# Dealing the next quarter's modulation out among the column groups of the first projection's tiles

## The chip, the cores and the metric

The kernel runs on one core of a Trainium2 chip. The metric is the device time of one execution in microseconds (us); lower is better. The engines named below are TensorE (PE), its weight loads (PEld), VectorE (DVE), ScalarE (ACT), GpSimd (POOL) and SyncE (SP), whose queue issues nearly all loads.

## The reference, cut to what matters

One block of a streaming encoder over 256 positions of 2048 channels. What the change touches is its beginning: the modulation vectors and the first projection.

```python
c_act = jax.nn.silu(c)
mod = c_act @ w_ada[l] + b_ada[l]                        # (2048) @ (2048, 6*2048)
sh_m, sc_m, gt_m, sh_f, sc_f, gt_f = split(mod, 6)
h = rms_norm(x, g_norm_mix[l]) * (1 + sc_m) + sh_m
proj = h @ w_in[l]                                       # conv B | conv C | conv h | q lat | kv lat | key
...                                                      # short convolution, latent attention, w_out
x = x + gt_m * (merged @ w_out[l])
h2 = rms_norm(x, g_norm_ffn[l]) * (1 + sc_f) + sh_f
x = x + gt_f * peer_ffn(h2, ...)                         # retrieval over 16384 experts
return rms_norm(x, g_final)
```

All of it is float32. The kernel numbers the modulation vectors 0 to 5 in the order of the split: 0 is the mixer's shift, 1 its scale.

## The kernel before

Positions lie along the free axis (256 columns), channels along the partitions, in 16 tiles of 128. A weight tile is 128 x 2048 float32 (1 MiB). Its product is exact to float32 by three matmuls: ACT writes a rounded copy `hwin` (L198), DVE the remainder `lwin` (L199), and PE multiplies hi by hi, hi by lo and lo by hi. `rwin`, `hwin` and `lwin` are the raw, high and low copies of a tile of `w_in`.

The first projection, called in0 here, can't wait for the whole modulation, since vectors 0 and 1 alone are 32 MiB of weights. It goes in four quarters (q = 0 to 3) of 512 channels. A quarter takes the modulation of its 512 channels, made by the generator `ada_q(q)`: for vector m = 1 and then m = 0 four loads of 1 MiB each (kg = 0 to 3, L393). Half of the 16 row blocks are multiplied by PE in column groups of 32 (L397, kg 1 and 3), half by DVE (L401, L403, kg 0 and 2); DVE folds PE's part in (L406), four narrow matmuls sum over the partitions (L408), and DVE adds the bias (L311, L314) into `modc`. With the scale DVE makes `xs` (L416), with the shift ACT and DVE make the quarter's activations `hhi` and `hlo` (`shift_split`, L355 and L356). Then PE adds the quarter's part of 12 column tiles: three weight tiles (g = 0 to 2) with four column groups (n) of 12 matmuls each (L669, L671, L676), accumulated in six PSUM banks `pin` over the four quarters. After each weight tile the loop takes `ADA_STEPS[g]` steps of the next quarter's `ada_q`.

The tile framework orders each engine's instructions: it takes the code's order as priority, raised for weight splits by `high_priority`, and each engine then runs its list strictly in that order. SP runs its loads in order too: a load whose place in memory is not yet free holds back all behind it. The pool `t8` has six places of 1 MiB: the raw modulation tiles `ada` use them, but `lat`, `lathi` and `latlo`, the latents that are written only after in0, are allocated ahead of the loop and hold three of the six. Raw weight tiles have four places (`WRAW`), `hwin` and `lwin` two each.

After in0 come the other projection tiles (`pwin`), the latents' norms (`lat_chain`: `lacc`, `ssl`, `rl0r` and `rl1r`, `rlb`), attention, convolution and the output projection (`pwout`). Beside them the modulation vectors 2, 4 and 3 are made by `ada_stream`, 16 loads each, one DVE product of 128 x 2048 per load (L239, L241); `feed(PACE)` takes the steps, PACE per projection tile. `ada_finish` sums such a vector over the partitions and turns it into columns.

```python
ADA_STEPS = (3, 3, 2)
ADA_LAST = (0, 1, 1)
PACE = (48 - sum(ADA_LAST)) / 43.0
ADA_PE = (4, 5, 6, 7, 12, 13, 14, 15)
```

Of the kernel before, what the change touches and what calls it, by code (L numbers as in the profile page):

```python
# [130 lines left out]
def hybrid_block_kernel(  # L131
# [111 lines left out]
    with tc.tile_pool(name="pre", bufs=1) as pre:  # L243
# [10 lines left out]
        zsel = pre.tile([128, 31], F32, name="zsel")  # L254
        V.memset(zsel, 0.0)
        V.memset(zsel[:, 15:16], 1.0)
# [50 lines left out]
        def ada_cols(m, c0, src):  # L307
# [3 lines left out]
            V.tensor_tensor(dst, src, vec[:, b:b + n], ALU.add)  # L311
# [75 lines left out]
        def ada_q(q):  # L387
            for m in (1, 0):
                acc = s2(f"acc{m}_{q}")
                prow = ps_tile(f"adarow{m}_{q}")  # L390
                for kg in range(4):
                    raw = t8(f"ada{m}_{q}_{kg}", shape=(128, 4, 512))
                    nc.sync.dma_start(raw.rearrange("p a b -> p (a b)"), w_ada01[q, 1 - m, kg])  # L393
                    for j in range(4):
                        k = 4 * kg + j
                        if k in ADA_PE:
                            PE.matmul(prow[32 * j:32 * j + 32], lhsT=cact[:, k:k + 1].to_broadcast([128, 32]),  # L397
                                      rhs=raw[:, j], start=(k == ADA_PE[j]), stop=(k == ADA_PE[j + 4]),
                                      tile_position=(0, 32 * j))
# [27 lines left out]
        lat = t8("lat")  # L427
        lathi = t8("lathi", F32R)
        latlo = t8("latlo", F32R)
# [208 lines left out]
        def after_in0(g):  # L638
            tick()
            if g < 2:  # L640
# [8 lines left out]

        for _ in ada_q(0):  # L650
            pass
        for q in range(4):
            nxt = ada_q(q + 1) if q < 3 else ada
            ws0 = {}
            for g in range(NG0):
                for gg_ in range(g, min(NG0, g + (2 if q == 3 else 1))):
                    if gg_ not in ws0:
                        ws0[gg_] = load_split(w_in0[gg_, q], f"win0_{gg_}_{q}")
                whi, wlo = ws0[g]
                if g == 0:  # L660
                    for j in range(4):
                        c = 4 * q + j
                        shift_split(xsv[q][j // 2][:, j % 2], modc[:, 0, c:c + 1], h[0][:, c], h[1][:, c])
                for n in range(4):
                    dst = pin[2 * g + n // 2][:, (n % 2) * 256:(n % 2) * 256 + 256]
                    for j in range(4):
                        c = 4 * q + j
                        sl = slice((4 * n + j) * 128, (4 * n + j + 1) * 128)
                        PE.matmul(dst, lhsT=whi[:, sl], rhs=h[0][:, c],  # L669
                                  start=(c == 0 and n % 2 == 0), stop=False, skip_group_check=True)  # L670
                        PE.matmul(dst, lhsT=whi[:, sl], rhs=h[1][:, c], start=False, stop=False,  # L671
                                  skip_group_check=True)
                    for j in range(4):
                        c = 4 * q + j
                        sl = slice((4 * n + j) * 128, (4 * n + j + 1) * 128)
                        PE.matmul(dst, lhsT=wlo[:, sl], rhs=h[0][:, c], start=False, stop=(c == 15),  # L676
                                  skip_group_check=True)
                if q == 3:
# [736 lines left out]
```

## Time and profile before

| | us |
|---|---|
| median of 3 runs | 1780.37 |
| lowest and highest | 1776.81, 1781.57 |
| the profiled execution, own time | 1774.11 |
| its span | 1771.5 |
| PE busy in it | 1679.7 (95%) |
| DVE busy | 1210.0 (68%) |

The profiled execution is the one all rows below come from. Its own time is 2.6 us over its span and 6.3 us under the median of the three runs. Dates are microseconds from the start of the span. In0 ends at 167, the output projection at 473; what follows, to the end, is the retrieval. Busy time is an average over stages that are limited by different things, so each stage is read by itself.

### The profile page before, as it was taken

Reading aid. Unit: us, or ns where it says so; the run is one execution under the profiler, and the core shown is the slowest. Engines: PE = TensorE matmul, PEld = TensorE weight load, DVE = VectorE, ACT = ScalarE, POOL = GpSimd, SP = SyncE. Lnnn points to the kernel's source line nnn. Section 1 sums busy time; section 2 is a strip of 40 time slices with the busy share of each in tenths; the row PEclk is TensorE's granted clock in tenths of the full one; section 3 lists DMA queues with packets and bytes.
Section 4 is the critical chain, followed back from the end, with each engine's and each line's share of the span. In section 5 each row is a group of like instructions: output and inputs, shape, how many; then the busy total and the mean of one; then the engine's idle time right before and its main releaser. Section 6 shows DMA issues by size and latency. Waiting matters only on the chain.

```text
span 1771.5 us, 29562 instructions
## 1 busy us (share of the span) xinstructions
PE 1679.7 (95%) x12526; PEld 1461.9 (83%) x12526; DVE 1210.0 (68%) x1621; ACT 761.3 (43%) x1013; POOL 297.5 (17%) x257
## 2 busy tenths in 40 slices
PE   3777999999999999999999999999999999999996
PEld 2667999989999999899999999999999854444542
DVE  6667978979867898898876697898754232312424
ACT  3224356534544449856884433333333232312322
POOL 0000000000000000000001000000030377777771
PEclk8888999999999999999999999999999999999999
DMA  9986887869854555545659887878888699999895
GB/s 392 385 336 214 327 299 269 316 250 348 311 213 165 192 194 191 206 166 191 223 214 337 305 296 262 298 286 309 289 300 335 216 386 382 347 383 344 343 371 232
DMA packets 77928, 505.93 MB, mean 286 GB/s; under 512 B 9472, under 2 KB 10112, under 8 KB 22496
## 3 DMA queue, kind: packets, MB, share of 16 engines
q1 hardware_dynamic: 44784, 319.82, 48.4%
q0 software_dynamic: 29712, 162.94, 25.1%
q10 hardware_dynamic: 3296, 21.24, 3.0%
q8 instruction: 100, 1.64, 0.4%
q14 instruction: 36, 0.29, 0.0%
HBM read 466.21 MB, written 37.75 MB: 284 GB/s over the span
## 4 chain that ended last, share of the span: by engine, by line
PE 85%; DVE 7%; ACT 4%; DMA 2%; issue 1%; POOL 1%; POOLq 0%; SPq 0%; ACTq 0%; DVEq 0%
PE pu L213 13%; PE pu L214 13%; PE pu L217 13%; PE po L1203 11%; PE po L1211 6%; PE gps L857 2%; PE pwin L213 2%; PE pwin L214 2%; PE pq L213 2%; PE pq L217 2%; PE pq L214 2%; DVE lwin L199 2%; PE pwout L213 1%; PE pwin L217 1%; PE pwout L214 1%; PE pwout L217 1%
## 5 line engine op out<-in xcount | busy, mean ns | idle before, releaser
L213 PE MATMUL pu<-h2hi,hu 128*128 128x256 f32 x2048 | 497.8, 285 | 0.0
L198 ACT ACTIVATE hu<-ru 128x2048 fp32r<-128x2048 f32 x128 | 245.5, 1918 | 364.4 <-PE pu L214 310.4
L213 PEld LDWEIGHTS pu<-h2hi,hu 128*128 128x128 f32 x2048 | 385.9, 188 | 0.6 <-issue 0.2
L199 DVE TENSOR_TENSOR lu<-ru,hu 128x2048 fp32r<-128x2048 f32 x128 | 292.9, 2289 | 134.4 <-ACT hu L198 134.2
L217 PE MATMUL pu<-h2hi,lu 128*128 128x256 f32 x2048 | 263.0, 281 | 0.0
L217 PEld LDWEIGHTS pu<-h2hi,lu 128*128 128x128 f32 x2048 | 251.3, 189 | 0.0
L214 PE MATMUL pu<-h2loT3a,hu 128*128 128x256 f32 x1024 | 249.7, 282 | 0.0
L214 PE MATMUL pu<-h2loT3b,hu 128*128 128x256 f32 x1024 | 248.2, 281 | 0.0
L1203 PE MATMUL po<-rv,mc 128*64 128x512 f32 (+2 forms) x1064 | 219.9, 595 | 5.1 <-PEq L1285 2.6
L214 PEld LDWEIGHTS pu<-h2loT3a,hu 128*128 128x128 f32 x1024 | 193.8, 189 | 0.2 <-issue 0.2
L214 PEld LDWEIGHTS pu<-h2loT3b,hu 128*128 128x128 f32 x1024 | 193.6, 189 | 0.0
L1203 PEld LDWEIGHTS po<-rv,mc 128*64 128x64 f32 (+2 forms) x1064 | 69.3, 129 | 144.5 <-issue 136.3
L1100 POOL DMA_DIRECT2D gg<-gd x16 | 18.7, 1170 | 928.5 <-DMA gd<-stage 928.3
L1152 POOL DMA_INDIRECT mc<-actd,perm_idx x109 | 134.4, 1233 | 37.1 <-issue 30.8
L1145 POOL DMA_INDIRECT rv<-in_peer_v_dram,perm_idx x107 | 125.3, 1171 | 65.5 <-issue 25.3
L204 DVE TENSOR_TENSOR lv<-rv,hv 128x2048 fp32r<-128x2048 f32 x24 | 55.1, 2295 | 117.5 <-ACT hv L203 117.4
L241 DVE SCALAR_TENSOR_TENSOR acc<-ada,cact,acc 128x2048 f32<-128x2048 f32 x45 | 105.7, 2349 | 5.9 <-DMA ada<-in_w_ada_dram 5.9
L203 ACT ACTIVATE hv<-rv 128x2048 fp32r<-128x2048 f32 x24 | 45.9, 1913 | 125.6 <-DMA rv<-in_peer_v_dram,perm_idx 98.1
L198 ACT ACTIVATE hwin<-rwin 128x2048 fp32r<-128x2048 f32 x33 | 63.1, 1916 | 81.3 <-DMA rwin<-in_w_in_dram 46.1
L204 DVE TENSOR_TENSOR third<-rv,third 128x2048 fp32r<-128x2048 f32 x12 | 27.5, 2294 | 89.5 <-ACT third L203 89.5
L847 ACT ACTIVATE oh<-oh,gT 128x128 f32<-128x128 f32 x256 | 80.9, 392 | 14.8 <-DVE oh L844 14.1
L213 PE MATMUL pwin<-hhi,hwin 128*128 128x256 f32 x336 | 84.7, 293 | 0.0
(522 smaller groups left out, 3048.1 us busy)
## 6 DMA issues: line engine op xcount, KB each, us to landing
ru<-in_peer_u_dram SPq DMA_DIRECT2D x128, 1024.0 KB, 5.3
ada<-in_w_ada_dram SPq DMA_DIRECT2D x96, 1024.0 KB, 6.7
rwin<-in_w_in_dram SPq DMA_DIRECT2D x33, 1024.0 KB, 6.1
rwout<-in_w_out_dram SPq DMA_DIRECT2D x16, 1024.0 KB, 7.3
rwq<-in_w_q_dram SPq DMA_DIRECT2D x16, 1024.0 KB, 6.5
gd<-stage ACTq DMA_DIRECT2D x16, 1024.0 KB, 5.3
gg<-gd POOLq DMA_DIRECT2D x16, 1024.0 KB, 11.1
actd<-A POOLq DMA_DIRECT2D x15, 1024.0 KB, 6.3
```

What stands on the lines that cost most here:

```text
L198: S.activation(hi, raw, AF.Copy)
L199: V.tensor_tensor(lo, raw, hi.bitcast(F32), ALU.subtract)
L204: V.tensor_tensor(lo, src, hi.bitcast(F32), ALU.subtract)
L213: PE.matmul(dst, lhsT=whi[:, sl], rhs=rhi[:, c], start=(c == sets[0][0]), stop=False)
L214: PE.matmul(dst, lhsT=whi[:, sl], rhs=rlo[:, c], start=False, stop=False)
L217: PE.matmul(dst, lhsT=wlo[:, sl], rhs=rhi[:, c], start=False, stop=(c == sets[-1][-1]))
L241: V.scalar_tensor_tensor(acc, raw, cact[:, k:k + 1], acc, ALU.mult, ALU.add)
L847: S.activation(ohs[1][:, j], ohs[1][:, j], AF.Copy, scale=gT[:, t + j:t + j + 1])
L1145: keep(nc.gpsimd.indirect_dma_start(raw, None, v_rows, index(main[n])))
L1152: keep(nc.gpsimd.indirect_dma_start(ms[-1][:, n % 8], None, actd[:, :], index(main[n])))
L1203: keep(PE.matmul(po[tt * 4 + d4][row:row + size], lhsT=m[:, at * size:(at + 1) * size], rhs=raw[:, d4 * 512:(d4 + 1) * 512], start=start, ...
L1211: keep(PE.matmul(po[tt * 4 + d4], lhsT=m[:, mi, tt * 128:(tt + 1) * 128], rhs=r[:, d4 * 512:(d4 + 1) * 512], start=False, stop=False, skip ...
```

## The change

The modulation of quarter q + 1 is no longer stepped between weight tiles but between column groups: after column group u (0 to 11) `UNITS[u]` steps are taken. The four matmul groups of a column group are a function, `unit`; the very first column group of a quarter does its products in the order hi by hi, low weights, low activations. The weight tile after the present one is split at the beginning of the present one (`take0`), across quarters too. PE takes 2 of 4 loads for the scale (kg 1 and 3) and 3 of 4 for the shift (kg 1 to 3). The latents are allocated after the first weight tile of the last quarter, so that the raw modulation tiles have six places. `PACE` rises from 46/43 to 46/41 per projection tile. `ada_finish` sums by four column groups of PE and four narrow matmuls instead of 16 matmuls and a transpose, with ACT copying between.

```diff
-ADA_STEPS = (3, 3, 2)
 ADA_LAST = (0, 1, 1)
-PACE = (48 - sum(ADA_LAST)) / 43.0
-ADA_PE = (4, 5, 6, 7, 12, 13, 14, 15)
+PACE = (48 - sum(ADA_LAST)) / 41.0
+ADA_PE = {1: (1, 3), 0: (1, 2, 3)}
+UNITS = {1: 1, 2: 1, 3: 1, 4: 1, 6: 1, 7: 1, 8: 2, 9: 1, 10: 1}
...
+        def by_columns(p, lhs, src, start=False, stop=False):
+            for j in range(4):
+                PE.matmul(p[32 * j:32 * j + 32], lhsT=lhs, rhs=src[:, j * 512:(j + 1) * 512], start=start, stop=stop,
+                          tile_position=(0, 32 * j))
+
         def ada_finish(m, acc):
             p = ps_tile(f"adaps{m}")
-            for j in range(16):
-                PE.matmul(p[:16, :128], lhsT=zsel[:, 15 - j:31 - j], rhs=acc[:, j * 128:(j + 1) * 128],
-                          start=(j == 0), stop=(j == 15))
+            by_columns(p, ones[:, 0:32], acc, True, True)
             row = s2(f"adarow{m}")
-            V.tensor_copy(row[:16, :128], p[:16, :128])
+            S.activation(row, p, AF.Copy)
             yield
-            PE.transpose(p[:, 256:272], row[:16, :128], ident[:16, :16])
-            ada_cols(m, 0, p[:, 256:272])
+            pc = ps_tile(f"adacol{m}")
+            for i in range(4):
+                PE.matmul(pc[:, 4 * i:4 * i + 4], lhsT=row[:, i * 128:(i + 1) * 128], rhs=quad4, start=True, stop=True)
+            ada_cols(m, 0, pc[:, 0:16], 4)
...
                         k = 4 * kg + j
-                        if k in ADA_PE:
+                        if kg in on_pe:
...
                 V.scalar_tensor_tensor(acc, prow, quad, acc, ALU.mult, ALU.add)
+                yield
...
-        lat = t8("lat")
-        lathi = t8("lathi", F32R)
-        latlo = t8("latlo", F32R)
+        lat = lathi = latlo = None
...
         for _ in ada_q(0):
             pass
+        ws0 = {0: take0(0)}
         for q in range(4):
             nxt = ada_q(q + 1) if q < 3 else ada
...
+            for u in range(4 * NG0):
+                g, n = divmod(u, 4)
+                i = NG0 * q + g
+                if n == 0 and i + 1 < 4 * NG0:
+                    ws0[i + 1] = take0(i + 1)
+                unit(q, g, n, ws0[i])
+                if q < 3:
+                    for _ in range(UNITS.get(u, 0)):
+                        next(nxt, None)
+                elif n == 3:
                     after_in0(g)
-                for _ in range((ADA_STEPS if q < 3 else ADA_LAST)[g]):
-                    next(nxt, None)
+                    for _ in range(ADA_LAST[g]):
+                        next(nxt, None)
```

Two places show what this does to the lists. The first is SP's list, the loads of the last quarter of in0. In a name the first number is the quarter of an `ada` tile, the second its kg, and for `rwin` the weight tile and then the quarter. Before:

```order
L393 DMA ada_3_0_805<-in_w_ada_dram 128x2048
L393 DMA ada_3_1_811<-in_w_ada_dram 128x2048
L393 DMA ada_3_2_817<-in_w_ada_dram 128x2048
L187 DMA rwin_1_2_823<-in_w_in_dram 128x2048
L393 DMA ada_3_3_877<-in_w_ada_dram 128x2048
L393 DMA ada_3_0_898<-in_w_ada_dram 128x2048
L393 DMA ada_3_1_904<-in_w_ada_dram 128x2048
L187 DMA rwin_2_2_910<-in_w_in_dram 128x2048
L393 DMA ada_3_2_964<-in_w_ada_dram 128x2048
L393 DMA ada_3_3_970<-in_w_ada_dram 128x2048
L187 DMA rwin_0_3_982<-in_w_in_dram 128x2048
```

After:

```order
L187 DMA rwin_1_2_755<-in_w_in_dram 128x2048
L401 DMA ada_3_0_787<-in_w_ada_dram 128x2048
L401 DMA ada_3_1_805<-in_w_ada_dram 128x2048
L401 DMA ada_3_2_823<-in_w_ada_dram 128x2048
L187 DMA rwin_2_2_829<-in_w_in_dram 128x2048
L401 DMA ada_3_3_847<-in_w_ada_dram 128x2048
L401 DMA ada_3_0_904<-in_w_ada_dram 128x2048
L187 DMA rwin_0_3_910<-in_w_in_dram 128x2048
L401 DMA ada_3_1_928<-in_w_ada_dram 128x2048
L401 DMA ada_3_2_934<-in_w_ada_dram 128x2048
L401 DMA ada_3_3_952<-in_w_ada_dram 128x2048
```

The weight tiles have moved one to three loads ahead; the number of loads of a quarter, eight of `ada` and three of `rwin`, is the same.

The second is DVE's list just after in0, around the norm of the first latent (`rl0v`, `rl0r`; `lacc` is its sum of squares, `acc` with `ada` a product of modulation vector 2, `lwin` the low copy of a weight tile). Before:

```order
L199 TENSOR_TENSOR lwin_1223<-rwin_1220,hwin_1222 128x2048
L338 RECIPROCAL rl0r<-rl0r 128x2
L446 TENSOR_TENSOR lacc_1127<-lsq_1126 128x256
L339 SCALAR_TENSOR_TENSOR rl0v<-rl0v,rl0r 128x2
L465 TENSOR_TENSOR krT<-kraw,rope_t 128x256
L340 TENSOR_TENSOR rl0v<-rl0v,rl0r 128x2
L447 TENSOR_TENSOR lacc_1127<-lacc_1127 128x256
L341 SCALAR_TENSOR_TENSOR rl0r<-rl0v,rl0r 128x2
L241 SCALAR_TENSOR_TENSOR acc_1133<-ada_2_1292,cact,acc_1133 128x2048
```

After:

```order
L199 TENSOR_TENSOR lwin_1226<-rwin_1223,hwin_1225 128x2048
L345 RECIPROCAL rl0r<-rl0r 128x2
L472 TENSOR_TENSOR krT<-kraw,rope_t 128x256
L346 SCALAR_TENSOR_TENSOR rl0v<-rl0v,rl0r 128x2
L526 MEMSET z_1215 128x2
L241 SCALAR_TENSOR_TENSOR acc_1136<-ada_2_1295,cact,acc_1136 128x2048
L347 TENSOR_TENSOR rl0v<-rl0v,rl0r 128x2
L527 TENSOR_TENSOR z_1215<-cs_1213,pin_179 128x256
L348 SCALAR_TENSOR_TENSOR rl0r<-rl0v,rl0r 128x2
```

A modulation product of 128 x 2048 now stands ahead of `rl0r`; further on, the low copy of a weight tile stands ahead of the second latent's `rl1r` where it stood behind. From the end of the output projection on, the lists of all engines are the same as before.

## Rows read from the trace of the kernel before

**Rows 1.** The page's line of DMA share, tenths in 40 slices of 44.3 us.

```profile
DMA  9986887869854555545659887878888699999895
```

**Rows 2.** Stretches of in0: engines' busy time, granted clock, DMA share, GB/s.

```profile
4.00:82.00 78.00, 45.85 (x282) 35.36 (x283) 53.47 (x91) 20.03 (x31) 0.00 (x0) 0.82 1.00 413
82.00:150.00 68.00, 52.83 (x370) 44.47 (x369) 44.23 (x59) 14.67 (x14) 0.00 (x0) 0.87 0.71 275
...
75.00:111.00 36.00, 28.97 (x194) 24.71 (x194) 23.34 (x29) 7.65 (x9) 0.00 (x0) 0.82 0.90 351
```

**Rows 3.** Waits of SP's queue from 40 to 150: total us, times, longest.

```profile
SPq L393 <- DVE acc L403: 43.8, 7, 9.8
SPq L187 <- DVE lwin L199: 27.0, 3, 13.1
```

**Rows 4.** ACT in time: start, us, what, idle before it and its releaser.

```profile
32.17 1.91 ACT L198 ACTIVATE hwin<-rwin 128x2048 fp32r<-128x2048 f32 x1 [14.00 <-DMA rwin<-in_w_in_dram]
...
42.12 1.92 ACT L198 ACTIVATE hwin<-rwin 128x2048 fp32r<-128x2048 f32 x1 [3.42 <-DMA rwin<-in_w_in_dram]
...
71.80 0.91 ACT L355 ACTIVATE hhi<-xs1a,modc 128x256 fp32r<-128x256 f32 x2 [17.17 <-DVE modc L311]
...
109.29 0.91 ACT L355 ACTIVATE hhi<-xs2a,modc 128x256 fp32r<-128x256 f32 x2 [15.14 <-DVE modc L311]
...
143.95 0.91 ACT L355 ACTIVATE hhi<-xs3a,modc 128x256 fp32r<-128x256 f32 x2 [14.65 <-DVE modc L311]
```

**Rows 5.** The chain of waits at the third quarter's start: start, us, what.

```profile
106.13 1.04 PE adarow L397 x8
107.20 0.76 DVE acc L406
108.00 1.07 PE adarow L408 x8
```

**Rows 6.** DVE's groups up to 170: count, busy us, mean ns, idle before.

```profile
L403 DVE SCALAR_TENSOR_TENSOR acc<-ada,cact,acc 128x512 f32<-128x512 f32 x56 | 42.1, 751 | 1.7
L199 DVE TENSOR_TENSOR lwin<-rwin,hwin 128x2048 fp32r<-128x2048 f32 x13 | 29.8, 2289 | 2.1 <-ACT hwin L198 2.1
...
L241 DVE SCALAR_TENSOR_TENSOR acc<-ada,cact,acc 128x2048 f32<-128x2048 f32 x2 | 4.7, 2349 | 0.0
```

**Rows 7.** The chain behind in0, two projection tiles at full clock.

```profile
183.24 1.89 PE pwin L217 x16
188.91 1.89 PE pwin L217 x16
```

**Rows 8.** PE in time in the second quarter, a wait and a matmul after.

```profile
75.36 0.58 PE L669 MATMUL pin<-hhi,hwin 128*128 128x256 f32 x1 [3.79 <-ACT hwin L198]
...
76.16 0.42 PE L671 MATMUL pin<-hlo,hwin 128*128 128x256 f32 x1
```

**Rows 9.** PE in time where in0 ends and the latents begin.

```profile
166.94 0.61 PE L347 MATMUL rlb<-ident,rl0r 128*128 128x128 f32 x4
...
167.75 0.36 PE L213 MATMUL pwin<-hhi,hwin 128*128 128x256 f32 x1
...
176.99 1.20 PE L347 MATMUL rlb<-ident,rl1r 128*128 128x128 f32 x4 [3.32 <-DVE rl1r L341]
```

**Rows 10.** DVE in time there.

```profile
165.58 0.42 DVE L447 TENSOR_TENSOR lacc<-lacc 128x256 f32<-128x256 f32 x1
165.91 0.16 DVE L341 SCALAR_TENSOR_TENSOR rl0r<-rl0v,rl0r 128x2 f32<-128x2 f32 x1
...
168.25 1.66 DVE L456 SCALAR_TENSOR_TENSOR lat<-lat,vec,rlb 128x256 f32<-128x256 f32 x4
...
172.43 1.23 DVE L204 TENSOR_TENSOR latlo<-lat,lathi 128x1024 fp32r<-128x1024 f32 x1
```

**Rows 11.** PE in time at the output projection's end.

```profile
472.66 3.67 PE L299 MATMUL adaps<-acc,zsel 128*16 128x128 f32 x32
...
477.03 0.61 PE L330 MATMUL x1ss<-ones,sacc 128*128 128x1 f32 x4
```

More of the change, by code (lines that the diff above doesn't have):

```diff
@@ L253, in hybrid_block_kernel @@
         perm = pre.tile([128, 128], F32, name="perm")
-        zsel = pre.tile([128, 31], F32, name="zsel")
-        V.memset(zsel, 0.0)
-        V.memset(zsel[:, 15:16], 1.0)
+        quad4 = pre.tile([128, 4], F32, name="quad4")
+        V.memset(quad4, 0.0)
+        for i in range(4):
+            V.memset(quad4[32 * i:32 * i + 1, i:i + 1], 1.0)
         quad = pre.tile([128, 1], F32, name="quad")
@@ L294, in drain, with ada_cols @@
                 tick()
+        def by_columns(p, lhs, src, start=False, stop=False):
+            for j in range(4):
+                PE.matmul(p[32 * j:32 * j + 32], lhsT=lhs, rhs=src[:, j * 512:(j + 1) * 512], start=start, stop=stop,
+                          tile_position=(0, 32 * j))
         def ada_finish(m, acc):
             p = ps_tile(f"adaps{m}")
[L298 to L300 removed]
+            by_columns(p, ones[:, 0:32], acc, True, True)
             row = s2(f"adarow{m}")
[L302 removed]
+            S.activation(row, p, AF.Copy)
             yield
[L304 to L307 removed]
+            pc = ps_tile(f"adacol{m}")
+            for i in range(4):
+                PE.matmul(pc[:, 4 * i:4 * i + 4], lhsT=row[:, i * 128:(i + 1) * 128], rhs=quad4, start=True, stop=True)
+            ada_cols(m, 0, pc[:, 0:16], 4)
+        def ada_cols(m, c0, src, k=1):
             n = src.shape[-1]
@@ L390, in ada_q @@
                 prow = ps_tile(f"adarow{m}_{q}")
+                on_pe = ADA_PE[m]
                 for kg in range(4):
@@ L395, in ada_q @@
                         k = 4 * kg + j
-                        if k in ADA_PE:
+                        if kg in on_pe:
                             PE.matmul(prow[32 * j:32 * j + 32], lhsT=cact[:, k:k + 1].to_broadcast([128, 32]),
-                                      rhs=raw[:, j], start=(k == ADA_PE[j]), stop=(k == ADA_PE[j + 4]),
+                                      rhs=raw[:, j], start=(kg == on_pe[0]), stop=(kg == on_pe[-1]),
                                       tile_position=(0, 32 * j))
@@ L638, in after_in0 @@
         def after_in0(g):
+            nonlocal lat, lathi, latlo
             tick()
+            if g == 0:
+                lat, lathi, latlo = t8("lat"), t8("lathi", F32R), t8("latlo", F32R)
             if g < 2:
@@ L648, in after_in0, with unit, one @@
                 spawn(rope(krT, kraw[:, :256], "kr", kr_place))
+        def unit(q, g, n, w):
+            whi, wlo = w
+            dst = pin[2 * g + n // 2][:, (n % 2) * 256:(n % 2) * 256 + 256]
+            first = q == 0 and n % 2 == 0
+            def one(j, wt, ht, start=False, stop=False):
+                PE.matmul(dst, lhsT=wt[:, (4 * n + j) * 128:(4 * n + j + 1) * 128], rhs=ht[:, 4 * q + j],
+                          start=start, stop=stop, skip_group_check=True)
+            if g == 0 and n == 0:
+                for j in range(4):
+                    one(j, whi, h[0], first and j == 0)
+                for j in range(4):
+                    one(j, wlo, h[0])
+                for j in range(4):
+                    one(j, whi, h[1], False, q == 3 and j == 3)
+                return
+            for j in range(4):
+                one(j, whi, h[0], first and j == 0)
+                one(j, whi, h[1])
+            for j in range(4):
+                one(j, wlo, h[0], False, q == 3 and j == 3)
@@ L650, in hybrid_block_kernel, with take0 @@
+        def take0(i):
+            return load_split(w_in0[i % NG0, i // NG0], f"win0_{i % NG0}_{i // NG0}", 0)
         for _ in ada_q(0):
             pass
+        ws0 = {0: take0(0)}
         for q in range(4):
             nxt = ada_q(q + 1) if q < 3 else ada
[L654 to L678, printed above, removed]
@@ new lines, in hybrid_block_kernel @@
+            for j in range(4):
+                c = 4 * q + j
+                shift_split(xsv[q][j // 2][:, j % 2], modc[:, 0, c:c + 1], h[0][:, c], h[1][:, c])
+            for u in range(4 * NG0):
[8 more added lines that the diff above has]
+                elif n == 3:
```

3 lines of the change are left out of this document (2 added, 1 removed).

## The prediction

> **What bounds the kernel now.** I read the load share over the whole span first [rows 1]: the loads are at 0.9 and more in the first two slices and fall to 0.6 to 0.8 in the third and fourth, which are still in0 (it ends at 167). So the span's beginning has two halves, and the stretches show them [rows 2]: from 4 to 82 the loads run at 413 GB/s with a share of 1.00; from 82 to 150 at 275 GB/s with 0.71. PE is busy for 45.85 of the first 78 us and 52.83 of the next 68, DVE for 53.47 and 44.23. No engine is full in the second half, and neither are the loads: this is a chain of waits. What holds the loads back stands in SP's own waits [rows 3]: 43.8 us for DVE's modulation products and 27.0 us for the low copies, that is, for places in memory to come free. What PE waits for stands on ACT [rows 4]: the quarters' activations begin at 71.80, 109.29 and 143.95, each after 15 to 17 us in which ACT waited for `modc`. A quarter takes (143.95 - 71.80)/2 = 36.1 us.
>
> The same quarter's work is far shorter on each engine. PE: three weight tiles at 188.91 - 183.24 = 5.67 us [rows 7] are 17.0; four modulation groups of 1.04 and two sums of 1.07 [rows 5] are 6.3; together 23.3. Loads: eleven tiles of 1 MiB. The 9th tile in the list behind `xt` starts its high copy at 32.17 and the 13th at 42.12, both straight from the load [rows 4], so 2.49 us per tile (1.049 MB at 413 GB/s [rows 2] is 2.54); I use 2.5, and a quarter is 27.5. The bound that is left when the waits go is the loads', 8.6 us per quarter below the present time.
>
> **The change part by part.** *Places and dealing out.* Six places for raw modulation tiles instead of three mean that a load waits for the tile six back. In the new list every such tile is used 5 us or more before its successor's load has to start, if loads follow each other without a gap: DVE's products are four or eight per vector at 0.75 [rows 6] and the PE groups now stand inside the weight tiles of the quarter before. DVE has per quarter 12 products (9.0), three low copies at 2.29 (6.9) [rows 6] and some 5 us of folds, `xs` and `hlo`: 21, under 27.5. PE has one group more than before: 5 x 1.04 + 2 x 1.07 + 17.0 = 24.3, under 27.5 too. So I let the loads run at 2.5 us to the end of in0. The last shift tile of the last quarter is the 42nd; three small tables of 832 KB stand between (0.8 tiles, 2.0 us). It lands at 32.17 + 33 x 2.5 + 2.0 = 116.7. From the start of its PE group to the activations' start it was 109.29 - 106.13 = 3.2 us in the third quarter [rows 4, 5], so the last quarter's activations begin at 119.9 instead of 143.95: 24.1 us earlier. The first quarter starts as before (its modulation is ready 2 us earlier, but a high copy of 1.9 now stands among its activations on ACT); the second starts at about 67 by DVE's list, not by the loads, which changes nothing behind it.
>
> *The last quarter.* Before, it took 166.94 - 143.95 = 23.0 [rows 4, 9], where three tiles at full clock are 17.0 and the first activation 0.9: 5.1 were lost to waiting for low activations and a low clock. The three tiles' high and low copies are ready a tile ahead now, but the wait in front of the first tile stays. I take a loss of 2.0: in0 ends at 119.9 + 0.9 + 17.0 + 2.0 = 139.8, a gain of 27.1. With a loss of 0 to 5.1 the gain is 29.1 to 24.0.
>
> *The latents behind it.* Here the new order costs something. DVE writes the last low copy of in0 when the first tile of the quarter frees the place for its high copy: 119.9 + 0.9 + 5.7 + 0.7 for that tile, 1.9 for ACT [rows 4], 2.3 for DVE, 131.4. Behind it up to `rl0r` stand four `lacc` sums, `krT` and `z` at 0.42, two products of 2.35, one low copy of 2.29 and five tiny operations of 0.16 [rows 6, 10]: 10.3. With 0.6 for ACT's next high copy, `rl0r` is ready at 142.3. PE needs it as soon as in0 ends, at 139.8, and waits 2.5; before, `rl0r` was done at 166.07, before PE came [rows 9, 10]. PE's projection begins 0.8 later, at 143.1 instead of 167.75: the gain is 24.7. From `rl0r` to `rl1r` the list is `lat` (1.66), `latlo` (1.23), two low copies (4.58), one product (2.35), two tiny operations to begin with and three more (0.8), and four operations on `ym` (some 1.7): 12.3, plus 0.2. PE asks after one tile (5.9), at 149.0, and gets it at 154.8: a wait of 5.8, where it was 3.32 [rows 9]. The gain at that point is 176.99 - 154.8 = 22.2. Bounds: with no new wait 27, and with PE at its low level for 3 us after each wait 19.
>
> *The long stretch to the output projection.* PE's list is the same tile for tile. DVE's products come 46/41 instead of 46/43 per tile, 0.05 x 2.35 = 0.1 us more per 5.67 us tile, and so end two tiles earlier. The same number in all, so I take 0; since DVE is nearly full beside some tiles, plus or minus 3.
>
> *`ada_finish`.* 16 matmuls took 3.67 [rows 11]. Four column groups are of the modulation groups' form (1.04 [rows 5]) and four narrow matmuls with 128 x 128 weights of the sums' form (1.07): 2.1. Two of the three finishes stand in PE's full stretch: 2 x 1.6 = 3.2 gained. The third stood between the output projection and `x1ss`, 477.03 - 472.66 = 4.4; it moves into the stretch (2.1 lost), and in its stead PE waits for the last residual and its square (0.9), a low copy that stands ahead on DVE (2.3) and the sum: 3.6. Sum: 3.2 + 4.4 - 2.1 - 3.6 = 1.9; bounds 0 and 4. Behind it the lists are the same, and the gain is carried to the end.
>
> **The sum.** 27.1 - 2.4 - 2.5 + 1.9 = 24.1 us. Against the profiled execution's own 1774.1 that is 1750.0; this execution lies 6.3 under the median of the three runs, so against the median of 1780.4 it is 1756.
>
> **A rule against it.** The loads' rate carries the sum. The rows show 413 GB/s over 78 us, with short stalls in it [rows 2]. The Trainium skill, in "DMA: Bandwidth & Descriptors", under "Where 436 GB/s comes from", says that for loads from HBM the memory side binds, at about 358 GB/s. By that figure a tile would take 2.93 us and the last shift tile would land at 131.2, 14.5 later, and the sum would be 9.6 instead of 24.1. The trace disagrees with it here. Its mechanism is the second rival.
>
> **The rivals.** (1) *The clock stays low.* PE starts a quarter after a wait; after 3.79 us of waiting its matmuls are listed at 0.42 [rows 8], the lower of the clock's two levels (1.2 and 2.4 GHz), at which a matmul takes twice the 1.89/16 = 0.118 of the upper one [rows 7], and the mean clock in in0 was 0.82 to 0.87 [rows 2]. If shorter waits at every group, now that PE's list is cut by modulation work that waits for loads, held PE at its low level, a quarter's PE work would be 48.6 instead of 24.3. It decides from the point where that passes 36.1, which is when half of the work is at the low level. With all of it there, two quarters would cost 12.5 each, the last one 11 and the second one's start nothing: 36 lost, less 2 for `ada_finish`, 1808 against the profiled execution and 1814 against the median. Against it: the waits that I find in the new list are 1 to 1.5 us each, not 3.8. (2) *The loads don't keep 2.5 us*, because a place comes free late or the rate is that of 75 to 111, 351 GB/s [rows 2], 2.99 us per tile. The last shift tile then lands at 32.17 + 33 x 2.99 + 2.4 = 133.2, 16.5 later, and the gain is 7.6: 1773. The stretch with 351 GB/s had SP waiting for places, though, so this needs the six places to be too few. (3) *DVE's list behind in0 costs more*: the two waits on `rl0r` and `rl1r` grow by another high copy each (1.9) and DVE doesn't catch up in the full stretch (3 more): a gain of 17, 1763. (4) *It costs nothing*, since PE and DVE interleave better than I lay them out: no new waits, gain 29, 1751. (5) *The change doesn't do what it says.* It does: the lists show the weight splits ahead and the modulation within the tiles, only the shift's three groups stand in a row at the quarter's end.
>
> **How the numbers follow.** My forecast, a gain of 20 to 28 (1752 to 1760), 0.56; rival 3 (1760 to 1768) 0.18; rival 4 (below 1752) 0.13; rival 2 (1768 to 1778, half of it within 0.3% of no change) 0.09; rival 1 0.04. A measurement of this kernel can tell 0.3%, 5.3 us, from no change. Faster: 0.56 + 0.18 + 0.13 + 0.04 = 0.91; same 0.05; slower 0.04. The range leaves out rival 1, most of rival 2 and the far ends: 1747 to 1767.
>
> **What would show it.** In the changed profile the loads should stay at a share of 1.00 and over 400 GB/s from 4 to about 120. ACT's activations should begin near 67, 93 and 120. PE's first projection tile behind in0 should begin near 143, and PE should wait 2 to 3 us for `rl0r` and 5 to 6 for `rl1r`. `x1ss` should begin at about 453. If the loads fall below 400 GB/s before 110, the places were too few and rival 2 holds; if PE's clock is below 0.8 between 65 and 140 with the loads not full, rival 1 does. If the activations begin at 120 but `x1ss` later than 460, the gain went in the stretch between.

## The result and the profile after

The kernel after takes 1760.6 us (median of 1756.7 to 1763.8) against 1778.6 for the kernel before: a ratio of 0.990, with a 95% interval of 0.987 to 0.992. That is 18.0 us faster; forecast were 24.1 us, 1756, with a range of 1747 to 1767. So the sign and the range hold, and a quarter of the gain is missing. The profiled execution took 1762.56 (span 1760.8). One execution of the experiment old_pace took 9373 us and is left out of its ratio.

The page's load share of after, in tenths of 40 slices of 44.0 us, answers to [rows 1]:

```profile
DMA  9998888679555455546569887888988599998895
```

The third slice was 8 and is 9, the fourth was 6 and is 8. The stretches answer to [rows 2]; the columns are length, the busy time of PE, weight load, DVE, ACT and POOL with instructions, granted clock, DMA share and GB/s:

```profile
4.00:82.00 78.00, 55.85 (x388) 42.53 (x389) 54.35 (x87) 22.14 (x33) 0.00 (x0) 0.91 1.01 425
82.00:120.00 38.00, 34.79 (x279) 28.28 (x277) 27.86 (x41) 8.94 (x8) 0.00 (x0) 0.95 1.01 426
120.00:141.00 21.00, 20.20 (x149) 20.12 (x149) 14.96 (x22) 12.51 (x17) 0.00 (x0) 0.84 0.74 282
```

The loads are full to 120, at 425 GB/s where the second half of in0 had 275, and PE's granted clock rose from 0.82 and 0.87 to 0.91 and 0.95. (The Trainium skill, in "DMA: Bandwidth & Descriptors", under "Where 436 GB/s comes from", says that some 358 GB/s bind loads from HBM, and works that figure out as half of what two cores share; here the kernel runs on one core, and these rows are 19% above it.) The quarters' activations on ACT, in time (start, us, what, idle before and its releaser), answer to [rows 4]:

```profile
64.78 0.91 ACT L362 ACTIVATE hhi<-xs1a,modc 128x256 fp32r<-128x256 f32 x2 [10.17 <-DVE modc L317]
...
92.27 0.91 ACT L362 ACTIVATE hhi<-xs2a,modc 128x256 fp32r<-128x256 f32 x2 [8.66 <-DVE modc L317]
...
120.41 0.91 ACT L362 ACTIVATE hhi<-xs3a,modc 128x256 fp32r<-128x256 f32 x2 [9.87 <-DVE modc L317]
```

Forecast were 67, 93 and 119.9. Up to here the prediction is met within 0.5 us at the last one: 23.5 us gained. From here on the gain shrinks. PE in time where in0 ends, and at `x1ss`, answers to [rows 9] and [rows 11]:

```profile
143.93 1.20 PE L354 MATMUL rlb<-ident,rl0r 128*128 128x128 f32 x4 [2.67 <-DVE rl0r L348]
144.91 0.85 PE L337 MATMUL ssl<-ones,lacc 128*128 128x1 f32 x4
145.63 0.56 PE L213 MATMUL pwin<-hhi,hwin 128*128 128x256 f32 x1
145.99 0.41 PE L214 MATMUL pwin<-hlo,hwin 128*128 128x256 f32 x1
...
151.71 2.06 PE L217 MATMUL pwin<-hhi,lwin 128*128 128x256 f32 x16
156.41 0.68 PE L354 MATMUL rlb<-ident,rl1r 128*128 128x128 f32 x4 [2.65 <-DVE rl1r L348]
...
460.69 0.60 PE L337 MATMUL x1ss<-ones,sacc 128*128 128x1 f32 x4 [3.11 <-DVE sacc L742]
```

PE waits 2.67 us for `rl0r`, then its matmuls are listed at 0.41, the lower level of the clock, until 150.5 (granted clock 0.50 from 143.9 to there), and it waits again. The second broadcast begins at 156.41 instead of 176.99: 20.6 gained. `x1ss` begins at 460.69 instead of 477.03: 16.3. At `gtfp`, a matmul late in the retrieval, it is 15.2 (1332.21 against 1347.43), and at `po`, the first matmul of the final stage, which reads rows for the experts, 14.4 (1387.57 against 1401.98). The two profiled executions differ by 10.7 in span, while the medians differ by 18.0. How that goes together stands at the end.

### The profile page after: what moved, and what is told of

It reads as the page before. It is cut to its first block, busy times and chain, and to the rows that moved or that the text cites. A ratio compares the mean times of both kernels' runs of the same rounds, so it can differ in the third digit from the quotient of the medians.

```text
span 1760.8 us, 29506 instructions
## 1 busy us (share of the span) xinstructions
PE 1683.4 (96%) x12507; PEld 1461.9 (83%) x12507; DVE 1200.5 (68%) x1605; ACT 761.6 (43%) x1016; POOL 288.1 (16%) x257
## 5 line engine op out<-in xcount | busy, mean ns | idle before, releaser
L1228 PE MATMUL po<-rv,mc 128*64 128x512 f32 (+2 forms) x1064 | 225.5, 600 | 5.2 <-PEq L1310 2.6
L1170 POOL DMA_INDIRECT rv<-in_peer_v_dram,perm_idx x107 | 129.1, 1207 | 77.1 <-PE po L1228 33.2
L1177 POOL DMA_INDIRECT mc<-actd,perm_idx x109 | 121.1, 1111 | 37.1 <-issue 30.8
L213 PE MATMUL pwin<-hhi,hwin 128*128 128x256 f32 x336 | 88.4, 301 | 0.0
```

The lines of the kernel that those rows point to most:

```text
L213: PE.matmul(dst, lhsT=whi[:, sl], rhs=rhi[:, c], start=(c == sets[0][0]), stop=False)
L1170: keep(nc.gpsimd.indirect_dma_start(raw, None, v_rows, index(main[n])))
L1177: keep(nc.gpsimd.indirect_dma_start(ms[-1][:, n % 8], None, actd[:, :], index(main[n])))
L1228: keep(PE.matmul(po[tt * 4 + d4][row:row + size], lhsT=m[:, at * size:(at + 1) * size], rhs=raw[:, d4 * 512:(d4 + 1) * 512], start=start, ...
```

## Experiments

Two dates in the trace carry the argument: when the last quarter's activations begin (in0) and when `x1ss` begins (all that the change touches). The table has both, the time between the latents' second broadcast and `x1ss` ("stretch"), and the ratio of times to the kernel before with its interval. The dates are those of one execution each. The runs were made in several sets, and the median of before lay between 1774.2 and 1779.5 us from set to set; so kernels of different sets are compared by their ratios and not by their times. The larger share of the modulation that PE takes and the order of products in a quarter's first column group are in every kernel made from after; neither was tried by itself.

| kernel | last activations | stretch | x1ss | ratio (95%) |
|---|---|---|---|---|
| before | 143.95 | 300.0 | 477.0 | 1 |
| after | 120.41 | 304.3 | 460.7 | 0.990 (0.987 to 0.992) |
| places_alone | 145.94 | 300.6 | 479.6 | 1.000 (0.999 to 1.001) |
| three_places | 120.26 | 304.8 | 460.9 | 0.991 (0.990 to 0.993) |
| no_split_ahead | 136.78 | 294.8 | 466.3 | 0.994 (0.992 to 0.995) |
| twelve_loads | 126.32 | 303.8 | 463.8 | 0.994 (0.993 to 0.995) |
| old_finish | 121.20 | 300.0 | 457.5 | 0.992 (0.990 to 0.993) |
| old_pace | 120.04 | 296.9 | 453.2 | 0.988 (0.986 to 0.990) |
| old_both | 121.11 | 301.5 | 458.8 | 0.988 (0.986 to 0.990) |
| pace_alone | 145.42 | 305.1 | 483.6 | 0.999 (0.997 to 1.001) |
| later_latents | 121.02 | 291.8 | 446.2 | 0.983 (0.981 to 0.984) |
| later_norms | 119.83 | 288.5 | 441.7 | 0.980 (0.978 to 0.982) |
| later_dense | 120.00 | 293.4 | 446.7 | 0.981 (0.979 to 0.984) |

### What makes in0 shorter

**places_alone**: the kernel before with six places.

```diff
-        lat = t8("lat")
-        lathi = t8("lathi", F32R)
-        latlo = t8("latlo", F32R)
+        lat = lathi = latlo = None
...
+            nonlocal lat, lathi, latlo
             tick()
+            if g == 0:
+                lat, lathi, latlo = t8("lat"), t8("lathi", F32R), t8("latlo", F32R)
```

> The kernel before, changed only so that the three latents' places are taken behind the first tile of in0's last quarter, which leaves six places for raw modulation tiles instead of three. Theory A (places and dealing out both needed, the places more): the loads run on while the modulation of the next quarter still stands between the tiles, a quarter falls from 36.1 us to 29 or 30, and the last quarter's activations begin near 131 instead of 144: 1765 us, some 14 faster than before. Rival B (the dealing out between column groups and the splits one tile ahead carry it): the activations begin within 4 us of 144 and the time stays at 1774 or more. Rival C (the places alone carry it): the activations begin at 122 or earlier, 1760.

Nothing is gained: the activations begin at 145.94, the time is that of before. SP's queue (waits from 40 to 150: total, times, longest) waits as in [rows 3]:

```profile
SPq L393 <- DVE acc L403: 45.2, 7, 9.8
...
SPq L187 <- DVE lwin L199: 23.6, 2, 13.1
```

The same products and low copies are waited for about as long as before (43.8 and 27.0). They free a place when they run, and they run when the order of the program lets them, between whole weight tiles. More places don't bring them forward.

**three_places** is the reverse: the kernel after with the three latents allocated at the start, the edit above undone.

> The kernel after, with the latents' places taken at the beginning again, so that three are left for raw modulation; dealing out, splits one tile ahead and everything else as after. Theory A: loads stop again for places, a quarter is 32 to 34 us, the last quarter's activations begin near 134, 1769 us. Rival B (dealing out carries it): within 3 us of after, 1761 to 1764. Rival C (places alone carry it): activations at 140 or later, 1776 or more.

In0 is that of after to 0.2 us (120.26) and so is `x1ss`. B holds. So the six places, the first thing that the prediction named, are worth nothing here.

**no_split_ahead**: the weight tile's load and split stand where the tile begins.

```diff
-                if n == 0 and i + 1 < 4 * NG0:
-                    ws0[i + 1] = take0(i + 1)
+                if n == 0 and i not in ws0:
+                    ws0[i] = take0(i)
```

> The kernel after, with in0's weights loaded and split when their own tile begins in the program, as before, and no longer one tile ahead; the dealing out between column groups stays. Theory A (the splits ahead take away the 13.0 us that PE waited for low copies and 3.8 for high ones in the kernel before, so both parts are needed): the last quarter's activations begin at 127 to 132 instead of 120.4, and the time is 1767 to 1772. Rival B (the dealing out alone carries the gain, as six places turned out not to): activations before 123, time within 3 us of after, 1761.

The activations begin at 136.78, 16.4 later: more than A had expected. PE's waits for high copies up to 145 (total, times, longest), here and then in after:

```profile
PE pin L666 <- ACT hwin L198: 14.8, 4, 3.8
```

```profile
PE pin L666 <- ACT hwin L198: 3.4, 1, 3.4
```

So the dealing out alone doesn't carry in0's gain: without the splits it gives 7.2 of 23.5 us. Whether the splits would do as well without the dealing out was not tried. (In the two lists of loads shown with the change, each weight tile stands three loads earlier, not one to three.) Yet `x1ss` is 5.6 later, not 16, since the stretch behind takes 294.8 instead of 304.3, and the ratio is 0.994 against 0.990, some 7 us, close to the 5.6 of the trace. That second finding is taken up below.

**ten_loads** leaves out one load of the shift in quarters 1 to 3 and computes its products from the scale's last tile; the modulation's values, and with them the experts chosen and the whole time (4088 us), are others, so only dates in in0 are read. **twelve_loads** loads one tile of each of these quarters a second time. The core of either:

```diff
-                    raw = t8(f"ada{m}_{q}_{kg}", shape=(128, 4, 512))
-                    nc.sync.dma_start(raw.rearrange("p a b -> p (a b)"), w_ada01[q, 1 - m, kg])
+                    if q == 0 or m == 1 or kg > 0:
+                        raw = t8(f"ada{m}_{q}_{kg}", shape=(128, 4, 512))
+                        nc.sync.dma_start(raw.rearrange("p a b -> p (a b)"), w_ada01[q, 1 - m, kg])
```

```diff
+                    if q > 0 and m == 0 and kg == 0:
+                        nc.sync.dma_start(ym.rearrange("p a b -> p (a b)"), w_ada01[q, 1, 1])
```

> The kernel after, with one load of 1 MiB left out in each of the quarters 1 to 3: the first raw tile of the shift is not loaded, its products use the last raw tile of the scale instead (so the modulation's values differ; all operations of the engines stay). Theory A (the loads set the quarter at 2.5 us per tile): each quarter is 2.5 us shorter, the last quarter's activations begin 7.5 us earlier, at 113, and the time is 1753. Rival B (PE's own 24.3 us with its waits of some 3 us for modulation and activations sets it just as much): the activations begin at 118 to 120.4 and the time is within 3 us of after.

> The kernel after, with one more load of 1 MiB in each of the quarters 1 to 3 (a raw modulation tile is loaded once more, into a buffer that in0 doesn't use; nothing reads it). With one load fewer the quarters became only 0.9, 0.9 and -0.1 us shorter. Theory A (loads and PE's list set the quarter at the same 27.5 us, so one more load shows in full): the last quarter's activations begin 6 to 7.5 us later, at 126.4 to 127.9, and the time is 1767 to 1768. Rival B (PE's list alone sets it and the loads have room): activations within 2 us of 120.4, time within 2 us of after.

One load fewer: the activations begin at 118.79, a gain of 1.6 of 7.5; B holds. One more: 126.32, a loss of 5.9 of 7.5; A's date holds but for 0.1. So the loads, at 2.5 us per tile, and PE's list both take about 27.5 us per quarter. PE's side can be seen in ten_loads, whose last shortened quarter has loads to spare (a share of 0.94, where it was 1.01 in the quarter ahead of it, which took 26.6) and is as long as that of after (28.1). These rows have the columns of the stretches above:

```profile
90.52:118.79 28.27, 25.88 (x200) 21.61 (x200) 20.26 (x28) 7.34 (x7) 0.00 (x0) 0.92 0.94 390
```

and PE at that quarter's end:

```profile
112.87 2.78 PE L407 MATMUL adarow<-ada,cact 128*32 128x512 f32 x24
117.25 1.31 PE L419 MATMUL adarow<-ones,acc 128*128 128x1 f32 x8 [1.60 <-DVE acc L416]
119.35 1.01 PE L668 MATMUL pin<-hhi,hwin 128*128 128x256 f32 x3 [0.79 <-ACT hhi L362]
```

PE is busy for 25.9 of 28.3 us; behind the shift's three groups in a row there is the chain of DVE's sum, PE's sums and the first activation. In twelve_loads `x1ss` is 3.1 later, so in its trace half of in0's 5.9 doesn't reach `x1ss`; the ratio, 0.994 against 0.990, some 7 us, doesn't show that half as saved.

### What takes the gain back

**old_pace** changes one number of after.

```diff
-PACE = (48 - sum(ADA_LAST)) / 41.0
+PACE = (48 - sum(ADA_LAST)) / 43.0
```

> The kernel after, with the later modulations dealt out at 46/43 products per tile as before instead of 46/41. Theory A (the denser products make DVE late for the attention's and the norms' short operations between 300 and 330, and PE's waits there cost its clock besides): the waits of 2.4 and 3.8 us at the attention's last transposes and at cn0b shrink to 0.9 and 2.3, 1757 us, 3 to 4 faster than after. Rival B (what is lost there comes from elsewhere, as from the finishes or from PE being earlier against the loads): the waits stay above 5 us in sum and the time is within 2 us of after.

`x1ss` begins at 453.2, where the prediction had put it (453), 7.5 earlier than after, 5.5 of it at the start of the output projection; most of the rest is the wait in front of `x1ss`, 0.3 instead of 3.1. The ratio is 0.002 to 0.003 under those of after and three_places, 3 to 6 us, with intervals that overlap. The two waits that A named are as A had them, 0.9 and 2.3, but there is a third, at `cn1b`. PE's waits there (total, times, longest):

```profile
PE cn1b L354 <- DVE cn1r L348: 2.6, 1, 2.6
PE cn0b L354 <- DVE cn0r L348: 2.3, 1, 2.3
...
PE at_4pn L634 <- DVE at_4on L626: 1.1, 2, 0.9
```

In after, from 284 to 345:

```profile
PE cn0b L354 <- DVE cn0r L348: 3.8, 1, 3.8
PE at_4pn L634 <- DVE at_4on L626: 2.4, 1, 2.4
```

The sums are 6.0 and 6.2, above the 5 us of B, so it isn't the waiting as such, and neither A nor B holds whole. What differs is the clock. Here are the same matmuls, from the attention's last tiles to `cn1b`, in before, in after, in old_pace and in no_split_ahead, with the columns of the stretches (the granted clock is the third figure from the end):

```profile
318.49:361.01 42.52, 37.48 (x304) 36.89 (x302) 38.42 (x66) 20.66 (x39) 0.00 (x0) 0.96 0.78 284
```

```profile
295.60:342.77 47.17, 40.98 (x299) 40.60 (x298) 35.14 (x64) 20.06 (x38) 0.00 (x0) 0.86 0.67 255
```

```profile
295.14:339.18 44.04, 39.01 (x305) 38.42 (x303) 38.54 (x66) 20.95 (x39) 0.00 (x0) 0.92 0.76 274
```

```profile
310.81:348.56 37.75, 35.16 (x299) 34.79 (x298) 34.49 (x64) 19.91 (x38) 0.00 (x0) 1.00 0.78 284
```

From before to after this piece grows by 4.7 us: PE is idle for 6.2 instead of 5.0, and the other 3.5 are the lower clock (0.86 instead of 0.96).

**pace_alone**, the kernel before with 41, was to show whether a dense pace costs by itself:

> The kernel before with 46/41 instead of 46/43 later modulation products per tile, and nothing else of the change. Theory A (denser products make DVE late for the attention's and norms' short operations wherever PE stands): PE's waits between 290 and 365 grow from 5.9 us by 2 or more, x1ss begins 3 to 7 us later than 477.0, the time is 3 to 7 us longer than before. Rival B (the pace costs only together with the earlier PE, or by the order that the scheduler happens to find): x1ss within 2 us of 477, or earlier.

Its profiled execution has `x1ss` 6.6 later, as A says, but that execution lies 4.8 above the median of its own kernel, and the ratio is 0.999. Over twelve runs the dense pace costs the kernel before nothing that can be measured: B, as far as times decide. Trace and times disagree here by more than the interval allows, and no run explains it; so a few us at `x1ss` in one trace are a sign and no measurement of the time.

**old_finish** brings back the 16 matmuls, the copy and the transpose of `ada_finish`; **old_both** does that with the old pace.

```diff
-            by_columns(p, ones[:, 0:32], acc, True, True)
+            for j in range(16):
+                PE.matmul(p[:16, :128], lhsT=zsel[:, 15 - j:31 - j], rhs=acc[:, j * 128:(j + 1) * 128],
+                          start=(j == 0), stop=(j == 15))
```

> The kernel after, with the old end of a modulation (16 matmuls of 128 columns, copy, transpose) in place of four column groups and four narrow matmuls. Theory A (the prediction's price: 1.6 us of PE for each of three finishes, all in the full stretch or in front of x1ss): x1ss begins 3.2 to 4.8 us later, at 464 to 465.5, and the time is 1764. Rival B (another order in the stretch weighs more than PE's 1.6): x1ss more than 2 us away from that on either side.

> The kernel after with the pace of before (46/43) and the old end of a modulation: of the change only in0's part is left. Theory A (the new end is worth what PE's list says, 2 to 3 us per finish, and with the pace of before no other order hides it): x1ss begins 4 to 7 us later than with the pace alone (453.2), at 457 to 460, 1758 to 1761 us. Rival B (PE's gain there is lost to DVE's order, as old_finish with the new pace was 3 us faster than after): x1ss within 2 us of 453.2, 1754 us.

The finish's price is as forecast or a little more: behind the first one the projection's tiles stand 2.0 us later in old_finish, relative to after (1.6 forecast). But `x1ss` begins 3.2 us earlier, since the stretch is 4.3 shorter; A falls. With the old pace it begins 5.6 later by the trace, as A had it, and the ratio is the same, as B had it. What the new finish is worth stays open, from a loss of 3 us to a gain of 6 by the traces.

What the stretch's length does depend on is seen best in after and no_split_ahead. From the second broadcast to `x1ss` both have the same matmuls and the same pace, and up to the first `at_4pn` (the attention's last transposes; 294.35 and 309.42) both take 137.9 us. At `cn1ss`, 336.20 and 341.99, they are 9.3 apart. Rows of after, then of no_split_ahead, with the columns of the stretches:

```profile
156.41:460.69 304.28, 290.84 (x2294) 283.20 (x2295) 255.88 (x299) 146.78 (x212) 0.00 (x0) 0.96 0.81 302
```

```profile
171.48:466.30 294.82, 285.06 (x2295) 277.20 (x2295) 257.81 (x302) 146.81 (x212) 0.00 (x0) 0.98 0.85 314
```

Of the 9.5 us, 3.7 are idle time of PE (13.4 against 9.8) and 5.8 are longer matmuls at a lower clock (0.96 against 0.98 as a mean). So the difference is made between these two points. From 310 to 330 of after the granted clock is 0.70:

```profile
310.00:330.00 20.00, 16.17 (x94) 16.00 (x95) 14.18 (x29) 4.96 (x12) 0.00 (x0) 0.70 0.64 253
```

ACT, then DVE in time ahead of `cn0b`, of after:

```profile
320.12 1.92 ACT L198 ACTIVATE hwin<-rwin 128x2048 fp32r<-128x2048 f32 x1 [6.60 <-PE pwin L214]
321.94 0.19 ACT L344 ACTIVATE cn0r<-cn0v 128x8 f32<-128x8 f32 x1
```

```profile
322.01 0.42 DVE L527 TENSOR_TENSOR z<-cs,pwin 128x256 f32<-128x256 f32 x1 [5.24 <-PE pwin L217]
322.35 0.20 DVE L345 RECIPROCAL cn0r<-cn0r 128x8 f32<-128x8 f32 x1
...
322.73 0.16 DVE L346 SCALAR_TENSOR_TENSOR cn0v<-cn0v,cn0r 128x8 f32<-128x8 f32 x1
322.81 2.28 DVE L199 TENSOR_TENSOR lwin<-rwin,hwin 128x2048 fp32r<-128x2048 f32 x1
325.01 0.16 DVE L347 TENSOR_TENSOR cn0v<-cn0v,cn0r 128x8 f32<-128x8 f32 x1
...
325.49 0.16 DVE L348 SCALAR_TENSOR_TENSOR cn0r<-cn0v,cn0r 128x8 f32<-128x8 f32 x1
```

DVE of no_split_ahead:

```profile
332.11 0.20 DVE L345 RECIPROCAL cn0r<-cn0r 128x8 f32<-128x8 f32 x1 [1.18 <-ACT cn0r L344]
...
333.52 0.15 DVE L347 TENSOR_TENSOR cn0v<-cn0v,cn0r 128x8 f32<-128x8 f32 x1
...
333.99 0.16 DVE L348 SCALAR_TENSOR_TENSOR cn0r<-cn0v,cn0r 128x8 f32<-128x8 f32 x1
334.07 2.28 DVE L199 TENSOR_TENSOR lwin<-rwin,hwin 128x2048 fp32r<-128x2048 f32 x1
```

And of before:

```profile
340.26 0.20 DVE L338 RECIPROCAL cn0r<-cn0r 128x8 f32<-128x8 f32 x1 [1.19 <-ACT cn0r L337]
...
342.14 0.16 DVE L341 SCALAR_TENSOR_TENSOR cn0r<-cn0v,cn0r 128x8 f32<-128x8 f32 x1
```

These four tiny operations take 2.0 us, from the first one's start to the last one's end, in no_split_ahead and in before, where only short ones stand among them, and 3.3 in after, where the scheduler has put a low copy among them. PE waits 3.8 instead of 2.3 us. Before that it waited 2.4 instead of 0.3 in front of the attention's last transposes, and the clock was low behind that wait. DVE isn't full at `cn0b`: ahead of `z` it had waited 5.24 us for the tile that PE was running. The chain begins so late because ACT's part of the norm, `cn0r`, stands behind a high copy that waits for the same tile. (The Trainium skill, in "Perfetto Trace Analysis", under "Tensor Engine Instruction (MATMUL, LD_WEIGHTS)", says that ACT, DVE and GpSimd work off their lists strictly in order; the rows agree: `cn0v` at 325.01, which needs nothing but DVE's own results, starts as the low copy of 322.81 ends.) The order is made when the program is built, and an edit ahead of the stretch can redraw it: among the kernels without later broadcasts the stretch takes 294.8 to 305.1. That the redrawn order makes the waits is read from the lists; no run changes the order alone.

**later_latents** tests the waits themselves: old_pace, with one pause more ahead of the latents' broadcast, so that PE has a weight tile to run meanwhile.

```diff
             r = rstd_cols(pl, 2, 512, f"rl{which}")
             yield
+            yield
```

> The kernel after with the pace of before (46/43), and the latents' broadcast matmuls one tile later in the program, so that PE has a tile to run while DVE finishes rl0r and rl1r. Theory A (the two waits of 2.7 us and the low clock behind them, some 2 us each, are lost at those two places and come back in full): x1ss begins 5 to 8 us earlier than with the pace alone (453.2), at 445 to 448, 1747 to 1749 us. Rival B (PE then waits for the next of DVE's results, the low copies or the latents, instead): less than 2 us earlier.

A's dates hold. Both waits are gone; PE in time:

```profile
147.87 0.61 PE L354 MATMUL rlb<-ident,rl0r 128*128 128x128 f32 x4
...
152.53 2.05 PE L217 MATMUL pwin<-hhi,lwin 128*128 128x256 f32 x16
154.42 0.61 PE L354 MATMUL rlb<-ident,rl1r 128*128 128x128 f32 x4
```

The latents' first use (`puq`) begins at 160.5 instead of 170.2, 9.6 earlier for two waits of 2.7, with the same matmuls ahead of it: the other 4.3 are the clock behind them. A new wait of 2.5 for a high copy takes some back, and `x1ss` is 7.0 earlier. The ratio to before is 0.983.

**later_norms** does the same for the conv norms (a pause in each, two begun one tile earlier); **later_dense** is after with both pauses and the dense pace.

```diff
             r = rstd_cols(sg, 2 * ng, 128, nm)
             yield
+            yield
...
-        15: [lambda: conv_norm(0, 4, "cn0")],
-        17: [lambda: conv_norm(4, 2, "cn1")],
+        14: [lambda: conv_norm(0, 4, "cn0")],
+        16: [lambda: conv_norm(4, 2, "cn1")],
```

> The kernel later_latents with the conv norms' broadcast matmuls one tile later too (a further pause in each, two of the three begun one tile earlier). Theory A (a short wait of PE costs itself and the low clock behind it, wherever it stands, and goes when PE has a tile to run): the waits at cn0b and cn1b, 2.3 and 2.2, go with some 1 to 2 us of clock each, and x1ss begins 5 to 8 us earlier than 446.2, 1735 to 1738 us. Rival B (DVE, nearly full between 270 and 310, hands its lateness on to the next wait): less than 2 us earlier.

> The kernel after with only the later broadcast matmuls of the latents and of the conv norms (as in later_norms), so with the dense pace of 46/41. Theory A (the dense pace costs only through PE's waits at the attention's last transposes, at cn0b and in front of x1ss): with the wait at cn0b gone, the ratio to before is within 0.002 of later_norms' 0.980, and x1ss begins within 3 us of 441.7 plus the wait of 3.1 that the dense pace leaves in front of it, 442 to 447. Rival B (the dense pace makes DVE late everywhere and costs its 3 to 6 us again): a ratio of 0.982 to 0.984, x1ss at 448 or later.

later_norms: the waits at `cn0b` and `cn1b` are gone and `x1ss` begins at 441.7, 4.6 earlier, between A and B and nearer to A; the broadcast behind `x1ss` waits 3.1 instead of 1.3. later_dense: 446.7 and 0.981, within A, at its edge. It differs from after by the pauses and the earlier start of two conv norms alone: the stretch falls from 304.3 to 293.4 and the ratio from 0.990 to 0.981. That is the test of the waits on the kernel after itself. All three are 1.7 to 2.0% faster than before and by their ratios 0.7 to 1.0% faster than after; their intervals overlap, so which is best is not settled.

## Why the prediction was right, and where it was not

**In0's bound: right size, wrong cause.** The quarter of 27.5 us and the last activations at 119.9 came out (120.4). But I had read [rows 3] as a lack of places, since SP waits "for places to come free". Three places do as well as six; that the date came out all the same is luck as far as the places go, since the same change brought the dealing out and the splits. The waits named the instruction that was late, and it was late by the order of the program, which the dealing out and the splits ahead mend. And the rate of the loads is no sole bound: PE's list, which I had at 24.3, comes to as much with the waits at the quarter's end, which I had left out of that sum (28.3 in the quarter of ten_loads that has loads to spare). One load fewer in each of three quarters brought 1.6 of 7.5 us, so faster loads alone would have brought little.

**The last quarter**: 20.85 instead of 19.9; a loss of 2.9 where 2.0 was assumed.

**The latents**: the wait for `rl0r` was 2.67 (2.5 forecast). The wait for `rl1r` was 2.65 and not 5.8, because the tile between ran at the low clock: it and the two small groups ahead of it took 156.41 - 143.93 - 2.65 = 9.8 where 6.7 was reckoned, and filled the wait. The date is DVE's, 156.4 where 154.8 was forecast, and the 1.6 come from in0: 0.5 at its last activations, 1.0 in the last quarter. A gain of 20.6, with 22.2 forecast.

**The step that failed is the long stretch**, taken as 0 plus or minus 3. Together with `ada_finish` it was to give 1.9 and it cost 4.2 (304.3 - 300.0): 6.1 of the 7.8 us that are missing at `x1ss`. My argument was that PE's list and the number of products are the same. They are. What counts is at which point of DVE's list, full beside the attention (97% from 270 to 310), the short operations stand that PE waits for, and what clock PE has behind the waits: up to the first `at_4pn` after is 2.8 us ahead of before, from there to the start of the output projection it takes 62.7 instead of 57.0, at a granted clock of 0.89 instead of 0.94 and with the same idle time of some 6 us, and from there to `x1ss` another 1.5 more, the wait of 3.1 among them. The prediction went through the lists no further than the latents, though the short operations had moved in them; how the clock would fall could not be read there. The finish itself came to 2.0 per piece and 3.1 for the last one's wait (1.6 and 3.6 forecast), so that term stands in the trace; the times don't tell it.

**The rivals.** The clock didn't stay low in in0 (0.91 to 0.95), the loads kept their rate. The third, that DVE's list costs more, gave 1763 with a band of 1760 to 1768, and the time of 1760.6 lies in that band and just outside my own of 1752 to 1760: it was right about the engine, and I had given it 0.18. Its two longer waits behind in0 (3.8 us) didn't come; its loss in the stretch, put at 3, came as 6.1 against the forecast. The prediction's own sign for that, activations at 120 and `x1ss` later than 460, is what the trace shows (120.4 and 460.7).

**14.4 or 18.0 us.** The dates give 14.4 up to the final stage; the medians give 18.0, 13.5 to 22.4 with the interval. That stage, with the same list of instructions, took from its first matmul to the end 369.5 us in the profiled execution of before, 373.2 in that of after and 380.9 in that of later_norms, which lies 9.9 over the median of its kernel. So the difference is within what this stage varies by.

## What to carry to other kernels

A wait for a place in memory names who holds it, not what is short: ask whether the holder is late for want of places or because of the order, and try the one without the other. A change far ahead of a stretch can reorder the lists of the engines that others wait for; look in the lists of that stretch, ACT's too, for short operations that PE waits for and that now stand behind long ones. The cheapest mend here was to give PE a tile to run before it asks for the result: one more pause in front of two broadcasts was worth 7.0 us at `x1ss` here, where the whole change brought 16.3.

## What the runs showed of the hardware

A wait of 2 to 3 us can cost PE as much again in clock, or nothing. Behind the wait of 2.67 at 143.93 in after the matmuls are listed at 0.41 until 150.5 (0.28 later on); the granted clock at 310 to 330, around two waits, is 0.70. Behind the wait of 2.3 at `cn0b` the granted clock of the next 6 us is 0.72 in before and in old_pace, and 1.00 in no_split_ahead; behind the wait of 2.6 at `cn1b` it is 0.74 in before and 1.00 in old_pace. So the length of a wait doesn't tell what it costs in clock, and what does is not shown here. Between after and no_split_ahead, 5.8 of 9.5 us of difference were clock and 3.7 waiting.

The final stage's length changes from one profiled execution to another with the same instructions; why is not shown. From the first `po` to the end, before and later_norms:

```profile
1401.98:1771.00 369.02, 351.20 (x1622) 167.50 (x1620) 113.30 (x111) 89.88 (x94) 250.76 (x210) 0.99 0.89 344
```

```profile
1371.44:1752.00 380.56, 359.71 (x1622) 171.08 (x1620) 113.05 (x111) 89.66 (x94) 240.16 (x210) 0.97 0.86 333
```

PE has the same 1622 rows and is busy for 8.5 us longer, at a clock of 0.97 instead of 0.99, and idle for 3.0 longer. So one profiled execution can mislead by 10 us about a kernel's time (that of later_norms lies 9.9 over the median of its kernel), and the date at which the changed part ends says more about that part than the span does.
